# Joining two expert plans into one, with the conditional moved from after the third expert pair to the last heavy expert's first product

## The chip, the cores and the metric

The kernel runs on one core of one Trainium2 chip. The metric is device time in microseconds (us) of one execution. The engines have short names: PE is the matrix engine, DVE the vector engine, ACT the scalar engine, POOL GpSimd, and SP the engine whose queue starts the weight loads.

## What is computed

The program is a two-layer backbone. Layer 0 has attention, a gated convolution and a dense SwiGLU; layer 1 has the same mixing part and then eight experts, of which each token uses two. The change touches only the experts:

```python
def moe_swiglu(h, w_router, w_gu, w_down):
    logits = (h @ w_router).astype(jnp.float32)
    top_v, top_i = lax.top_k(logits, TOP_K)
    top_w = jax.nn.softmax(top_v, axis=-1)
    gates = jnp.sum(jax.nn.one_hot(top_i, N_EXPERTS, dtype=jnp.float32) * top_w[..., None], axis=-2).astype(h.dtype)
    y = jnp.zeros_like(h)
    for e in range(N_EXPERTS):
        y = y + gates[..., e:e + 1] * swiglu(h, w_gu[e], w_down[e])
    return y
```

There are 256 tokens of width 1024; an expert has 1024 x 7168 gate and up weights and 3584 x 1024 down weights in float32, 42 loads of 1 MB each, so that all eight are 336 loads.

## The kernel before, in words

The experts are sorted by how many tokens chose them. The four fullest (ranks 0 to 3) are **heavy**: up to 128 tokens as the stationary operand, and every weight tile is split into a high and a low float32r half, so that one product becomes three (`mm3`, L535 to L537). The four emptiest (ranks 4 to 7) are **light**: up to 64 tokens, and the weights are used as they were loaded (`light_gu`, L1731, and `light_down`, L1799). Rank 1 may have up to 160 tokens. If it has more than 128, the rest of them, the **few**, are multiplied by the unsplit weights as well (L1707 and L1777, tokens prepared in `few_tokens`). A conditional on that count (`k1 > 8 * 128 + 7`, L1888) chooses between two copies of the code, one with the few and one without. The page shows products of L1707, so the copy with the few, which stands first, is the one that runs. An earlier conditional (L1873) guards all of this: its first branch is for other counts of tokens and does not run here; the plans stand in its far branch.

A heavy and a light expert form a pair. `schedule` writes the order of the work: the 3584 columns are cut into four chunks (1024, 1024, 1024, 512), and a step takes gate (`g`) and up (`u`) of one chunk of the heavy and one of the light expert, in turns, then down (`d`) of the chunk before, and the turn (`t`, transposes of the activation). With `LAG_L` = 1 the light expert runs one chunk behind the heavy one. Before the change there are two plans:

```python
HS, LS, LAG_L = (0, 2, 3), (4, 5, 6), 1
plans = [list(schedule(HS, LS, LAG_L)), list(schedule((1,), (7,), 0))]
```

Plan one runs three pairs with the lag, plan two the pair of ranks 1 and 7 without it, behind the conditional. The program order of the plan is kept on PE, DVE and ACT. Loads go through `Mixed`, in the plan's order, into eight raw buffers (`raw`). A heavy weight tile is split by a copy on ACT (`whi`, L99, two halves) and a subtraction on DVE (`wlo`, L100) into one of three buffers of each kind; its raw buffer is then free. A light tile's raw buffer is free when PE has read it, and a tile that the few also need is kept until then. `Wb.ready(2)` after every operation of the plan issues splits until two heavy tiles lie ready, and starts the loads that have become possible. Every engine works its list in order, so where a split stands in the list of ACT or DVE decides what waits behind it.

Small work is put between the operations by `bg_step`: `gather` and `light_gather` fetch the tokens of the next experts (selectors on DVE, products on PE, copies on ACT), and `combine` adds a finished expert into `y` (products on PE, L1359, sums on DVE, L1361). `finish` makes the last sums, the norm and the output.

Of the kernel before, what the change touches and what calls it, by code (L numbers as in the profile page):

```python
# [123 lines left out]
class Mixed(Stream):  # L124

    floor, cap = None, None

# [24 lines left out]
    def get(self, kind):  # L154
        i = self.gi
        assert self.items[i][1] == kind, (kind, self.items[i][1])
        self.load(i + 1)
        self.split(i + 1)
        self.more(i)
        self.gi += 1  # L160
        self.last_raw = self.kept.pop(i, None)
        return self.done.pop(i)
# [3 lines left out]
def kernel(ctx: ExitStack, tc: tile.TileContext, x, c, cx, c_ctx, w_ada, b_ada, norm_g,  # L166
# [855 lines left out]
    def schedule(hs, ls, lag):  # L1022
# [6 lines left out]
        for s in range(n + lag + 1):  # L1029
# [3 lines left out]
            for op in "gu":  # L1033
                for i in range(2):
                    for kind, at in (("H", H), ("L", L)):
                        if i in parts(at):
                            yield kind + op, *at, i
            last = s == n and not lag
            for i in range(2):
                for kind, at, new in (("L", LP, L), ("H", HP, H)) if last else (("H", HP, H), ("L", LP, L)):  # L1040
                    if i in parts(at):
                        yield kind + "d", *at, i
                    if new and i == max(len(parts(at)) - 1, 0):
                        yield kind + "t", *new, 0

    HS, LS, LAG_L = (0, 2, 3), (4, 5, 6), 1
    plans = [list(schedule(HS, LS, LAG_L)), list(schedule((1,), (7,), 0))]

# [566 lines left out]
    def light_gather(p):  # L1615

        n = LS.index(p) if p in LS else 3
        tl_ = ring.tile([128, 512], F32R, "x2", 2 + n % 2)
# [4 lines left out]
        for t in range(2):  # L1623
            V.tensor_scalar(sl[:, t, :].rearrange("p (g n) -> p g n", g=2),
                            iota[:, 0:64].unsqueeze(1).to_broadcast([128, 2, 64]), posms[:, t, p:p + 1], None,
                            op0=OP.is_equal)
        yield
        for h in range(2):
# [16 lines left out]
    def run_pairs(plan, few, todo):  # L1645
# [14 lines left out]
        def few_tokens(p):  # L1660
# [6 lines left out]
            for h in range(2):  # L1667
                pb, q = (facc, lacc)[h], slice(32 * h, 32 * h + 32)
                for i, (t, src) in enumerate(((0, hth), (0, htl), (1, hth), (1, htl))):
# [7 lines left out]
            for t in range(2):  # L1677
                PE.transpose(lb[:, 128 * t:128 * t + 128], sl2[:, t, :].bitcast(F32), ident)
            A.copy(st2, lb[:, :256])
            yield  # L1680
# [55 lines left out]
        def heavy_turn(p, c, i):  # L1736
            n = CHUNKS[c][1]
            for b in range(n // 512):
# [4 lines left out]
                V.tensor_tensor(tl[b], hb[b], th[b].bitcast(F32), op=OP.subtract)  # L1743
            if few:
                for j in range(n // 512):
# [9 lines left out]
        def heavy_down(p, c, i):  # L1755
            nb = CHUNKS[c][1] // 512
            final = c == len(CHUNKS) - 1
            Wb.floor = Wb.gi if few else None
            raws = []
            for t in range(2):  # L1760
# [8 lines left out]
                if final:  # L1769
                    bg_step(2)  # L1770
            if few:
                for t in range(2):
# [7 lines left out]
            if final:  # L1780
                bg_flush()
                OE[p] = split_out(pd)
                parts = [(ST[p], whole(OE[p]))]
                if few:
                    split_hl(th[1], tl[1], facc)
                    parts.append((st2, in_halves((th[1], tl[1]))))
                if p != 1:
                    bg.append(combine(gates[:, :, p], parts, wait=2))
                S_["parts"] = parts

        def light_down(p, c, i):
# [16 lines left out]
        for op, p, c, i in plan:  # L1808
            for f in todo.get((op, p, c, i), ()):
# [71 lines left out]
    with odd_arm.Else():  # L1881
# [6 lines left out]
        with tc.If(k1 > 8 * 128 + 7) as few_arm:  # L1888
            finish(gates[:, :, 1], run_pairs(plans[1], True, {}))
        back1()  # L1890
        with few_arm.Else():
            finish(gates[:, :, 1], run_pairs(plans[1], False, {}))
    touch([k for k in shared if k[0] != "raw"])
# [46 lines left out]
```

## Time and profile before

| | us |
|---|---|
| median of 3 runs | 1942.01 (1940.58 to 1945.11) |
| the profiled execution's own time | 1943.33 |
| its span, first to last instruction | 1941.5 |
| PE busy, share of the span | 1829.9, 94% |
| DVE busy | 947.3, 49% |
| ACT busy | 812.0, 42% |
| main DMA queue | 519.27 MB, 73.5% of 16 engines |

An engine that is busy 94% of the time need not be the limit all along: the stages have different limits, and a row of the trace says for each gap which instruction or transfer ended it. Device time is a little longer than the span, here by 1.8 us, since it also covers what lies before the first and behind the last instruction.

### The profile page before, as it was taken

How to read it: one execution, taken by the hardware profiler on the slowest of the kernel's cores; microseconds unless marked ns; L12 is line 12 of the kernel's file. 1: busy time of each engine (PE TensorE's matmuls, PEld its weight loads, DVE VectorE, ACT ScalarE, POOL GpSimd, SP SyncE). 2: the span in 40 equal slices, each digit the busy share in tenths (PEclk: the TensorE clock that was granted, in tenths of full speed). 3: DMA queues.
4: the chain of work that ended last, by engine and by line, in shares of the span. 5: the costliest groups of instructions: out<-in, count | busy, mean ns of one | idle time of the engine just before them, and what ended most of it. 6: DMA issues, size and time to landing. Idle time of an engine off the chain costs nothing. (4 is left out here: it accounts for less than half of the span.)

```text
span 1941.5 us, 23935 instructions
## 1 busy us (share of the span) xinstructions
PE 1829.9 (94%) x9321; PEld 1277.7 (66%) x9321; DVE 947.3 (49%) x1310; ACT 812.0 (42%) x1194; POOL 79.0 (4%) x139
## 2 busy tenths in 40 slices
PE   6999999999999999999779989999999996999997
PEld 3866679877777888877656646665565653555563
DVE  3345578222223757546745535556355543345443
ACT  3354456221112546446445444444344532244432
POOL 2200110000000000201200000000000000000001
PEclk9999999999999999999779999999999998999999
DMA  9956296545552647634249999999999999799993
GB/s 332 211 171 204 87 313 211 171 151 173 173 174 101 245 153 260 153 99 183 79 156 340 377 383 397 394 406 402 365 405 403 409 404 363 295 358 381 368 365 121
DMA packets 223761, 521.12 MB, mean 268 GB/s; under 512 B 30041, under 2 KB 83857, under 8 KB 223633
## 3 DMA queue, kind: packets, MB, share of 16 engines
q1 hardware_dynamic: 223152, 519.27, 73.5%
q8 instruction: 77, 1.26, 0.3%
q14 instruction: 52, 0.42, 0.1%
q10 hardware_dynamic: 480, 0.18, 0.0%
HBM read 518.31 MB, written 3.13 MB: 269 GB/s over the span
## 5 line engine op out<-in xcount | busy, mean ns | idle before, releaser
L100 DVE TENSOR_TENSOR wlor<-rawr,whir 128x1024 fp32r<-128x1024 f32 x336 | 392.3, 1220 | 310.9 <-ACT whir L99 310.3
L99 ACT CAST whir<-rawr 128x1024 fp32r<-128x1024 f32 x336 | 333.5, 1049 | 254.9 <-DMA rawr<-in_w_down_moe_dram 116.4
L100 DVE TENSOR_TENSOR wlo<-raw,whi 128x1024 fp32r<-128x1024 f32 x188 | 224.8, 1223 | 113.6 <-ACT whi L99 74.5
L99 ACT CAST whi<-raw 128x1024 fp32r<-128x1024 f32 x192 | 193.0, 1049 | 142.3 <-PE pg L536 40.3
L1731 PE MATMUL gur<-rawr,x32r 128*64 128x512 f32 (+1 forms) x1024 | 210.0, 557 | 14.6 <-ACT lar L1753 14.1
L535 PE MATMUL gur<-whir,xgr 128*128 128x512 f32 x448 | 182.5, 407 | 18.9 <-DVE tlr L1743 8.4
L536 PE MATMUL gur<-wlor,xgr 128*128 128x512 f32 x448 | 177.8, 397 | 2.3 <-DVE wlor L100 2.3
L537 PE MATMUL gur<-whir,xgr 128*128 128x512 f32 x448 | 177.0, 395 | 0.0
L1731 PEld LDWEIGHTS gur<-rawr,x32r 128*64 128x64 f32 x1024 | 70.6, 140 | 127.8 <-issue 103.2
L535 PEld LDWEIGHTS gur<-whir,xgr 128*128 128x128 f32 x448 | 85.7, 191 | 56.7 <-issue 18.8
L1799 PE MATMUL pd<-rawr,lar 128*64 128x512 f32 x448 | 101.6, 598 | 1.7 <-ACT lar L1753 1.7
L536 PEld LDWEIGHTS gur<-wlor,xgr 128*128 128x128 f32 x448 | 85.9, 192 | 19.7 <-DVE wlor L100 3.2
L537 PEld LDWEIGHTS gur<-whir,xgr 128*128 128x128 f32 x448 | 85.8, 192 | 18.6
L535 PE MATMUL pg<-hh,whi 128*128 128x512 f32 (+1 forms) x256 | 95.0, 372 | 0.0
L537 PE MATMUL pu<-hh,wlo 128*128 128x512 f32 (+1 forms) x256 | 93.0, 363 | 0.4 <-DVE wlo L100 0.4
L537 PE MATMUL pg<-hh,wlo 128*128 128x512 f32 (+1 forms) x256 | 93.1, 364 | 0.0
L535 PE MATMUL pu<-hh,whi 128*128 128x512 f32 (+1 forms) x256 | 92.9, 363 | 0.0
L536 PE MATMUL pg<-hl,whi 128*128 128x512 f32 (+1 forms) x256 | 92.9, 363 | 0.0
L536 PE MATMUL pu<-hl,whi 128*128 128x512 f32 (+1 forms) x256 | 92.8, 362 | 0.0
L943 DVE TENSOR_TENSOR act<-sg,pu 128x512 f32<-128x512 f32 (+1 forms) x32 | 19.8, 618 | 147.1 <-PE pu L537 128.7
L535 PE MATMUL py<-whi,ah 128*128 128x512 f32 x224 | 87.4, 390 | 0.0
L537 PE MATMUL py<-whi,al 128*128 128x512 f32 x224 | 86.8, 390 | 0.6 <-DVE al L548 0.6
(391 smaller groups left out, 2972.9 us busy)
## 6 DMA issues: line engine op xcount, KB each, us to landing
rawr<-in_w_gu_moe_dram SPq DMA_DIRECT2D x224, 1024.0 KB
rawr<-in_w_down_moe_dram SPq DMA_DIRECT2D x112, 1024.0 KB
raw<-in_w_ada_dram SPq DMA_DIRECT2D x48, 1024.0 KB
raw<-in_w_gu_dense_dram SPq DMA_DIRECT2D x32, 1024.0 KB
raw<-in_w_down_dense_dram SPq DMA_DIRECT2D x28, 1024.0 KB
raw<-in_w_in_dram SPq DMA_DIRECT2D x24, 1024.0 KB
raw<-in_w_out_dram SPq DMA_DIRECT2D x12, 1024.0 KB
BM<-rep SPq DMA_DIRECT2D x8, 512.0 KB
```

The lines of the kernel that those rows point to most:

```text
L99: nc.scalar.copy(hi[:, q], flat[:, q])
L100: (nc.gpsimd if g == "G" else nc.vector).tensor_tensor(lo[:, q], flat[:, q], hi[:, q].bitcast(F32), op=OP.subtract)
L535: PE.matmul(o, wh, mh, start=first, stop=False, skip_group_check=shared)
L536: PE.matmul(o, wh, ml, start=False, stop=False, skip_group_check=shared)
L537: PE.matmul(o, wl, mh, start=False, stop=last, skip_group_check=shared)
L943: V.tensor_tensor(act[f // 4][:, f % 4, s0:s0 + n], sg, pu, op=OP.mult)
L1731: PE.matmul(o[64 * g_:64 * g_ + 64, :], X32[p][:, kk, :], raw[:, k, w2 * g_:w2 * g_ + w2], start=kk == 0, stop=kk == KD - 1)
L1799: PE.matmul(lacc[64 * h:64 * h + 64, :], lt[:, 128 * j + 64 * g_:128 * j + 64 * g_ + 64], raw[:, f, hsl(h)], start=c == 0 and i == t == f ...
```

## The change

There is one plan for all four pairs, `schedule((0, 2, 3, 1), (4, 5, 6, 7), 1)`, cut in two lists at the first product of the last heavy expert. The conditional stands at the cut, so the last chunk of the third pair's light expert, and the down products of both its experts' last chunks, now lie behind the conditional, inside both copies. The last pair runs with the lag.

```diff
-    floor, cap = None, None
+    floor, cap, eager = None, None, False
...
         self.split(i + 1)
+        self.gi += 1
+        if self.eager:
+            self.ready(2)
         self.more(i)
-        self.gi += 1
...
-            last = s == n and not lag
             for i in range(2):
-                for kind, at, new in (("L", LP, L), ("H", HP, H)) if last else (("H", HP, H), ("L", LP, L)):
+                for kind, at, new in (("H", HP, H), ("L", LP, L)):
...
-    HS, LS, LAG_L = (0, 2, 3), (4, 5, 6), 1
-    plans = [list(schedule(HS, LS, LAG_L)), list(schedule((1,), (7,), 0))]
+    HS, LS, LAG_L = (0, 2, 3, 1), (4, 5, 6, 7), 1
+    plan = list(schedule(HS, LS, LAG_L))
+
+    cut = plan.index(("Hg", 1, 0, 0))
+    plans = [plan[:cut], plan[cut:]]
...
-        yield
+        yield from pause(3)
...
-                bg.append(combine(gates[:, :, p], [(SL32[p], in_halves(o))], wait=2 if p != 7 else 0))
+                S_["parts"] = [(SL32[p], in_halves(o))]
+                if p != LS[-1]:
+                    bg.append(combine(gates[:, :, p], S_["parts"], wait=2))
...
-            Wb.ready(2)
-            if op[1] != "t":
+            if after[0][1:] != "t":
+                Wb.ready(3 if op[0] == "L" else 2)
+
+            if op[1] == "d" or op[1] != "t" and not few:
                 bg_step(2 if (p, c) == (0, 0) else 1)
...
-            finish(gates[:, :, 1], run_pairs(plans[1], True, {}))
+            finish(gates[:, :, LS[-1]], run_pairs(plans[1], True, {}))
```

Further small edits go with it: the few are used only where `p == 1`, and their tokens are prepared in the heavy accumulators `hb` and in `facc`, since `lacc` and `lb` now hold the light expert's sums at that time; the heavy expert of rank 1 is combined in the background, and the light one of rank 7 in `finish`.

Splits move in three ways. After a light operation up to three heavy tiles are made ready, not two. No split is issued between an operation and a turn that follows it. In the first chunk of the first heavy expert (`eager`) splits are issued inside the products. The gather of the light tokens pauses for three more operations behind its selectors, and with the few the background work advances only behind down products.

**On ACT, at the conditional** (`thr` and `lar` are the turned activations of heavy and light, `whi` the split's high half, `rawr_7094` the raw buffer of the 245th load in both kernels). Before, from the last heavy down products' tiles on:

```order
L99 CAST whir_7102<-rawr_7096 128x1024 x2
L99 CAST whir_7216<-rawr_7094 128x1024 x2
L99 CAST whir_7385<-rawr_7096 128x1024 x2
L1742 CAST thr_7405<-gur_7409 128x512
L1753 COPY lar_7396<-gur_7411 128x512
L1720 ACTIVATE sgr_7401<-gur_7411 128x256
L547 CAST oer_7397<-pdn0r_7412 128x512
L547 CAST oer_7397<-pdn1r_7413 128x512
L99 CAST whir_7102<-rawr_7094 128x1024 x2
```

Now, up to the few's tokens (`sgr_7402`):

```order
L99 CAST whir_7102<-rawr_7096 128x1024 x2
L99 CAST whir_7216<-rawr_7086 128x1024 x2
L1746 CAST thr_7405<-gur_7409 128x512
L99 CAST whir_7385<-rawr_7088 128x1024 x2
L1757 COPY lar_7396<-gur_7411 128x512
L99 CAST whir_7102<-rawr_7094 128x1024 x2
L1895 COMPARE_AND_BRANCH
L1675 COPY sgr_7402<-gur_7409 32x512
L1675 COPY sgr_7402<-gur_7410 32x512
```

Both turns now stand ahead of that split; the conditional and the copies of the few's tokens stand behind it. The DVE list has the same order: the split's low half, the conditional, then the selectors of the few.

**On ACT, in the first heavy expert's first chunk** (`actr` is its activated gate, `x2f` the gathered light tokens). Before:

```order
L99 CAST whir_7102<-rawr_7092 128x1024 x2
L1632 COPY x2f<-pd_7383 64x512
L1720 ACTIVATE actr_7403<-gur_7409 128x512
L1720 ACTIVATE actr_7404<-gur_7410 128x512
L99 CAST whir_7216<-rawr_7094 128x1024 x2
L99 CAST whir_7385<-rawr_7096 128x1024 x2
L1632 COPY x2f<-tr_7382 64x512
L1637 CAST x2r_7392<-pd_7383 128x256
```

Now:

```order
L99 CAST whir_7102<-rawr_7092 128x1024 x2
L99 CAST whir_7216<-rawr_7094 128x1024 x2
L99 CAST whir_7385<-rawr_7096 128x1024 x2
L1724 ACTIVATE actr_7403<-gur_7409 128x512
L1724 ACTIVATE actr_7404<-gur_7410 128x512
L1636 COPY x2f<-pd_7383 64x512
L99 CAST whir_7102<-rawr_7098 128x1024 x2
L99 CAST whir_7216<-rawr_7100 128x1024 x2
```

Two tiles are split ahead of the gate's activation that were split behind it, and the copy of the light tokens moved behind it.

**On PE, at the second light gather** (`pd_7383` receives the gathered tokens, `gur_7411` is the light accumulator). Before, between two operations of the plan:

```order
L1731 MATMUL gur_7411<-rawr_7098,x32r_7394 64x512 x4
L1731 MATMUL gur_7411<-rawr_7100,x32r_7394 64x512 x4
L1631 MATMUL pd_7383<-hth,x2r_7393 128x512
L1631 MATMUL pd_7383<-htl,x2r_7393 128x512
L1631 MATMUL pd_7383<-hth,x2r_7393 128x512
L1631 MATMUL pd_7383<-htl,x2r_7393 128x512
L1731 MATMUL gur_7411<-rawr_7086,x32r_7394 64x512 x4
L1731 MATMUL gur_7411<-rawr_7088,x32r_7394 64x512 x4
```

Now:

```order
L538 MATMUL gur_7409<-wlor_7386,xgr_7387 128x512
L539 MATMUL gur_7409<-whir_7385,xgr_7387 128x512
L1635 MATMUL pd_7383<-hth,x2r_7393 128x512
L1635 MATMUL pd_7383<-htl,x2r_7393 128x512
L1635 MATMUL pd_7383<-hth,x2r_7393 128x512
L1635 MATMUL pd_7383<-htl,x2r_7393 128x512
L1735 MATMUL gur_7411<-rawr_7094,x32r_7394 64x512 x4
L1735 MATMUL gur_7411<-rawr_7096,x32r_7394 64x512 x4
```

The four products stand three operations further on, behind the next heavy gate or up products; their selectors on DVE stayed where they were.

## Rows read from the trace of the kernel before

**Rows 1.** The page's 40 slices of the span (48.5 us each): TensorE, then the DMA engines.
```profile
PE   6999999999999999999779989999999996999997
...
DMA  9956296545552647634249999999999999799993
```

**Rows 2.** Stretches of 50 us: us, PE, PEld, DVE, ACT, POOL busy, clock, DMA share, GB/s.
```profile
1300.00:1350.00 50.00, 50.00 (x222) 30.11 (x221) 25.44 (x25) 20.40 (x25) 0.00 (x0) 1.00 1.02 400
1600.00:1650.00 50.00, 34.89 (x178) 19.50 (x175) 15.78 (x15) 13.31 (x15) 0.00 (x0) 0.83 0.94 365
1650.00:1700.00 50.00, 46.23 (x242) 25.42 (x242) 18.53 (x24) 14.99 (x21) 0.00 (x0) 0.97 0.77 296
1750.00:1800.00 50.00, 50.00 (x289) 29.31 (x287) 26.91 (x27) 21.51 (x24) 0.00 (x0) 1.00 0.98 378
```

**Rows 3.** Timeline, PE, between the two plans: start, length, work, [idle before <- releaser].
```profile
1624.13 0.65 PE L1752 MATMUL gur<-kc,sgr 128*128 128x128 f32 x4
1638.87 6.11 PE L1731 MATMUL gur<-rawr,x32r 128*64 128x256 f32 x32 [14.08 <-ACT lar L1753]
...
1663.92 3.65 PE L1799 MATMUL pd<-rawr,lar 128*64 128x512 f32 x16 [1.23 <-ACT lar L1753]
...
1669.67 0.73 PE L1359 MATMUL pd<-oer,str 128*128 128x512 f32 x2 [0.95 <-DVE y L1361]
...
1674.78 0.80 PE L1670 MATMUL pd<-hth,x2r 128*128 128x512 f32 x1 [1.23 <-DVE p L1664]
```

**Rows 4.** Timeline, ACT, the same stretch.
```profile
1612.27 1.99 ACT L99 CAST whir<-rawr 128x1024 fp32r<-128x1024 f32 x2 [5.70 <-DMA rawr<-in_w_down_moe_dram]
...
1633.30 1.99 ACT L99 CAST whir<-rawr 128x1024 fp32r<-128x1024 f32 x2 [16.49 <-DMA rawr<-in_w_down_moe_dram]
1635.85 1.99 ACT L99 CAST whir<-rawr 128x1024 fp32r<-128x1024 f32 x2 [0.56 <-DMA rawr<-in_w_down_moe_dram]
...
1638.23 0.59 ACT L1753 COPY lar<-gur 128x512 f32<-128x512 f32 x1
```

**Rows 5.** Timeline, DVE: last split of plan one, first selector behind the conditional.
```profile
1634.38 2.36 DVE L100 TENSOR_TENSOR wlor<-rawr,whir 128x1024 fp32r<-128x1024 f32 x2 [16.12 <-ACT whir L99]
...
1674.26 0.14 DVE L1664 TENSOR_SCALAR p<-posms 128x1 f32<-128x1 f32 x1
```

**Rows 6.** Timeline, PE: the waits of the first pairs.
```profile
1000.22 0.50 PE L536 MATMUL gur<-wlor,xgr 128*128 128x512 f32 x1 [0.75 <-DVE wlor L100]
...
1017.55 0.79 PE L535 MATMUL gur<-whir,xgr 128*128 128x512 f32 x1 [4.48 <-DVE tlr L1743]
...
1147.92 0.79 PE L1631 MATMUL pd<-hth,x2r 128*128 128x512 f32 x1 [5.91 <-DVE x2r L1624]
...
1371.36 0.80 PE L1631 MATMUL tr<-hth,x2r 128*128 128x512 f32 x1 [4.20 <-DVE x2r L1624]
```

**Rows 7.** Stretches of 10 us around those waits, columns as in rows 2.
```profile
1010.00:1020.00 10.00, 5.39 (x22) 3.81 (x21) 9.01 (x10) 3.89 (x5) 0.00 (x0) 0.79 0.76 278
1150.00:1160.00 10.00, 10.00 (x39) 5.67 (x40) 0.00 (x0) 3.75 (x5) 0.00 (x0) 0.88 0.81 306
1370.00:1380.00 10.00, 8.64 (x24) 3.51 (x25) 1.50 (x3) 1.18 (x2) 0.00 (x0) 0.66 0.71 261
```

**Rows 8.** Timeline, PE, the end of the last pair.
```profile
1909.04 3.65 PE L1799 MATMUL pd<-rawr,lar 128*64 128x512 f32 x16 [0.47 <-ACT lar L1753]
...
1919.07 0.73 PE L1359 MATMUL tr<-x2r,x2r 64*128 64x512 f32 x2 [0.84 <-DVE y L1361]
...
1925.18 1.19 PE L1359 MATMUL gur<-oer,str 128*128 128x512 f32 x4
```

**Rows 9.** Timeline, ACT: a gate, and the split that is queued behind it.
```profile
1138.46 0.60 ACT L1720 ACTIVATE actr<-gur 128x512 f32<-128x512 f32 x1 [6.00 <-PE gur L537]
1141.53 1.99 ACT L99 CAST whir<-rawr 128x1024 fp32r<-128x1024 f32 x2 [2.47 <-DMA rawr<-in_w_gu_moe_dram]
```

**Rows 10.** Timeline, PE: the first product behind the first conditional.
```profile
982.43 0.80 PE L535 MATMUL gur<-whir,xgr 128*128 128x512 f32 x1 [6.80 <-issue]
```

More of the change, by code (lines that the diff above doesn't have):

```diff
@@ L1615, in light_gather @@
     def light_gather(p):
-        n = LS.index(p) if p in LS else 3
+        n = LS.index(p)
         tl_ = ring.tile([128, 512], F32R, "x2", 2 + n % 2)
@@ L1667, in few_tokens @@
             for h in range(2):
-                pb, q = (facc, lacc)[h], slice(32 * h, 32 * h + 32)
+                pb, q = hb[h], slice(32 * h, 32 * h + 32)
                 for i, (t, src) in enumerate(((0, hth), (0, htl), (1, hth), (1, htl))):
@@ L1677, in few_tokens @@
             for t in range(2):
-                PE.transpose(lb[:, 128 * t:128 * t + 128], sl2[:, t, :].bitcast(F32), ident)
-            A.copy(st2, lb[:, :256])
+                PE.transpose(facc[:, 128 * t:128 * t + 128], sl2[:, t, :].bitcast(F32), ident)
+            A.copy(st2, facc[:, :256])
             yield
@@ L1743, in heavy_turn @@
                 V.tensor_tensor(tl[b], hb[b], th[b].bitcast(F32), op=OP.subtract)
-            if few:
+            if few and p == 1:
                 for j in range(n // 512):
@@ L1757, in heavy_down @@
             final = c == len(CHUNKS) - 1
-            Wb.floor = Wb.gi if few else None
+            Wb.floor = Wb.gi if few and p == 1 else None
             raws = []
@@ L1770, in heavy_down @@
                     bg_step(2)
-            if few:
+            if few and p == 1:
                 for t in range(2):
@@ L1783, in heavy_down @@
                 parts = [(ST[p], whole(OE[p]))]
-                if few:
+                if few and p == 1:
                     split_hl(th[1], tl[1], facc)
                     parts.append((st2, in_halves((th[1], tl[1]))))
-                if p != 1:
-                    bg.append(combine(gates[:, :, p], parts, wait=2))
-                S_["parts"] = parts
+                bg.append(combine(gates[:, :, p], parts, wait=1 if p == 1 else 2))
         def light_down(p, c, i):
@@ L1803, in light_down @@
                 split_hl(*o, lacc)
-                bg.append(combine(gates[:, :, p], [(SL32[p], in_halves(o))], wait=2 if p != 7 else 0))
+                S_["parts"] = [(SL32[p], in_halves(o))]
+                if p != LS[-1]:
+                    bg.append(combine(gates[:, :, p], S_["parts"], wait=2))
         code = nc.cur_bb.bb.instructions
         n = len(code)
-        for op, p, c, i in plan:
+        for (op, p, c, i), after in zip(plan, plan[1:] + [("", 0, 0, 0)]):
+            Wb.eager = (p, c) == (0, 0)
             for f in todo.get((op, p, c, i), ()):
@@ L1888 @@
         with tc.If(k1 > 8 * 128 + 7) as few_arm:
-            finish(gates[:, :, 1], run_pairs(plans[1], True, {}))
+            finish(gates[:, :, LS[-1]], run_pairs(plans[1], True, {}))
         back1()
         with few_arm.Else():
-            finish(gates[:, :, 1], run_pairs(plans[1], False, {}))
+            finish(gates[:, :, LS[-1]], run_pairs(plans[1], False, {}))
     touch([k for k in shared if k[0] != "raw"])
```

## The prediction

> **What bounds the kernel now.** I read the page's slices first: from the 22nd slice on (about 1020 us) PE and the DMA engines are both at 9 or above, with one dip on PE at the 34th [rows 1]. That is the stage of the experts, the only one that the change touches. So the second view is busy time by stretch. In 1300 to 1350 PE is busy all the time and the DMA share is 1.02 at 400 GB/s: two limits of nearly the same height. In 1600 to 1700 PE loses 15.1 and 3.8 us and the DMA share falls to 0.77. From 1750 on PE is full and the DMA share is 0.98 at 378 GB/s: there PE is the limit, since the last pair also multiplies the few [rows 2].
>
> The third view is the timeline at the border of the two plans. PE ends the last light turn of plan one at 1624.13 + 0.65 and waits until 1638.87, for `lar`, a copy on ACT [rows 3]. The copy itself is short. It stands behind the splits of two tiles that had not landed: ACT waited 16.49 us for the first, cast it at 1633.30, the second at 1635.85, and only then came the turns [rows 4]. By the plan (three pairs of 84 loads, the last 12 of them light 4, heavy 2, light 6) these tiles are loads 245 and 246. Load 237, eight buffers before, was cast at 1612.27 [rows 4]: 21.0 us for eight loads is 2.63 us each, which is the DMA engines at their full pace. So up to the border the loads set the time, and PE waits for them wherever it gets ahead; behind it PE does, with hardly a gap up to 1909 [rows 8].
>
> The rule for the sum follows: ahead of the conditional only what lets loads start sooner counts; behind it, every microsecond that PE stands idle, and the moment at which it starts.
>
> **The restart at the border.** The new plan has the same 240 loads ahead of the cut, and the 245th, now the third tile of the last heavy expert, lands in the same place of the order. The turns move ahead of its split, but so does nothing else: split, conditional and the few's selectors and tokens follow in this order on ACT and DVE, and PE's next work is the tokens. With loads as before, the cast is at 1633.30, DVE ends the low half at 1634.38 + 2.36 = 1636.74 [rows 4, 5]. The first token product came 0.52 us after the first selector started (1674.78 against 1674.26) [rows 3, 5], so PE restarts at 1637.3, not 1638.87: **1.6 us gained**, where the diff looks as if it took away the whole wait of 14.08 [rows 3]. From here to the last product PE has the same products to make in either plan: light chunk, down products, tokens, the last pair. They only stand in another order.
>
> **The handshakes behind it.** Before, the combines of ranks 3 and 6 were flushed at the border, PE and DVE in turns, and then came the conditional and the tokens: waits of 1.23, 0.95 and 1.23 us [rows 3]. At the end 0.47 and 0.84 belong to the light turn and the combine of rank 7 among heavy products [rows 8]. Together 4.7 us. The eight parts of the two combines now stand singly behind down products. Their price is nothing if DVE's sum ends within the next down products, and 8 x 0.95 = 7.6 us if each waits as the one in the row did. I take 1.0, near nothing, because the next products of such a group are longer than the wait. **3.7 us gained.** In the tail the light combine of rank 7 now comes behind the last product where the heavy one of rank 1 was [rows 8]. There are four sums on DVE and the same norm in either case, so I put it at nothing, between a gain and a loss of 1.
>
> **The start.** In the first chunk PE waits 0.75 us for a low half and then 4.48 us for a turned activation's low half [rows 6]. The second stands on DVE behind splits that were issued between the products and the turn; these splits no longer go there, and the first is what the eager splits remove. In 1010 to 1020 the DMA share is 0.76 [rows 7]: the raw buffers are full and the loads follow PE, so what PE gains here the loads gain too. **5.0 us** of the 5.2. The ends are nothing, if the loads are held up again right after, and 8, if the clock of 0.79 in that stretch [rows 7] stays full as well.
>
> **The light gathers.** Twice PE stands at a gather's first product for a selector, 5.91 and 4.20 us [rows 6], because DVE built it behind the splits of tiles that had yet to land. Three operations later the selector is long done, so both waits go. But these stretches are bound by loads: what counts is the dip that follows, when PE had not freed the light buffers. The shares 0.81 and 0.71 against 1.02 are (0.21 + 0.31) x 10 = **5.2 us** [rows 2, 7]. The ends are nothing and the 10.1 us of the waits. The postponed copies are needed only when the next light expert starts, and that lies behind the rest of the step.
>
> The third tile ready after a light operation, and turns ahead of splits, cost nothing in themselves: the same casts in another order, on ACT and DVE which are half idle (in 1300 to 1350 busy 20.40 and 25.44 of 50 us) [rows 2].
>
> **Sum.** 1.6 + 3.7 + 5.0 + 5.2 = 15.5 us, so the profiled execution's 1943.33 would become 1927.8. That execution is 1.3 above the median of 1942.01; against the median I say **1926.5**. The loads' 10.2 us shift load 245, and with it the restart, to about 1627; the wait at the cut remains some 12 us long.
>
> **The rivals.**
> The loads don't gain. If the ring of eight buffers is held up at the next place, the two load terms are worth nothing, and 1.6 + 3.7 = 5.3 leaves 1936.7. For it: the share was 1.02 in most stretches, so a later bottleneck has little to give back. Against it: a dip in a full ring is time that nothing returns.
>
> More comes than that. If the third ready tile lets raw buffers go earlier all along, the upper ends count: 8 + 10.1 instead of 10.2, some 8 us more, 1918.5.
>
> Slower: a split in front of the gate. After a light operation the third split now stands ahead of the heavy gate's activation on ACT. In the trace a gate ran at 1138.46 and the split behind it waited 2.47 us for its load, to be cast in 1.99 up to 1143.52 [rows 9]. In the other order the gate would have been 1143.52 - 1138.46 = 5.1 us late. PE then waits for the accumulator that the gate empties, and the light buffers behind it go free later. The point from which it decides is three of the stage's some twelve steps, since 3 x 5.1 = 15.3 us eats the whole gain; if six steps lose that much, 6 x 5.1 - 15.5 = 15.1 us slower, about 1957. Against it: the up products that need the accumulator use that very tile, so PE mostly waits for it anyway.
>
> The conditional itself costs. At the first conditional, whose far branch runs, PE stood 6.80 us with no releaser in the profile [rows 10]; at the second one the gap of 1.23 ended with DVE's selector [rows 3], so I price it at nothing. If a gap like the first one came behind the wait at the cut, 1926.5 + 6.8 = 1933.3. The Trainium skill, "Runtime: NRT & Kernel Launch", section on instruction fetch mechanics, says that a taken branch to code outside the present window waits until that code is fetched. By that rule the jump into the far copy pays and falling into the near one does not; the trace agrees for both conditionals, 6.80 against none.
>
> **How the numbers follow.** Forecast 0.60 (its own range 1919 to 1933); loads don't gain 0.18 (1933 to 1940); more 0.10; slower 0.06; the conditional 0.06. A measurement of this kernel can tell about 0.2% from no change, 3.9 us, so faster means under 1938.1. The forecast, the larger gain and the conditional give 0.76 nearly whole, the second case about half: faster 0.85. Same has 0.08, the rest of the second case, and slower 0.07, the slower case and a little for losses that I have not seen. The range, 1916 to 1938, leaves out half of the larger gain (0.05), the part of the second case above 1938 (0.08) and the slower case (0.06), about 0.19.
>
> **What would show it.** Right: at the border one wait of PE, about 12 us, ended by DVE's selectors, with ACT's cast of the last split before the conditional near 1623; no wait for a selector at the gathers, and none over 2 us near 1015; shares near 1.02 where they were 0.81 and 0.71; PE without gaps from the tokens on. Wrong: the cast at the cut still near 1633 (the loads gained nothing), no wait at the cut (PE was the limit after all), gates on ACT behind a split that waits for a load while PE stands, or new gaps at the combines.

## The result, and the profile after

The changed kernel takes **1917.28 us** (median of 4 runs, 1915.79 to 1919.9), the kernel before in the same comparison 1943.56 us (1940.58 to 1947.96): a ratio of **0.9866, 95% interval 0.9845 to 0.9887**. The profiled execution of after took 1916.19 us with a span of 1914.4, against 1943.33 and 1941.5 before: 27.1 us less, where the sum said 15.5. In the changed file the lines lie a few numbers further down: a light product of L1731 is now L1735, down L1799 is L1801, the turns L1742 and L1752 are L1746 and L1756, the few's selectors L1664 are L1668, their token products L1670 are L1674, a combine's L1359 and L1361 are L1363 and L1365, and the split's L535 to L537 are L537 to L539.

The page's slices of after:

```profile
PE   6999999999999999999779999999999996999997
...
DMA  9956286645552656733438999999999998898994
```

The dip of PE at the 34th slice is still there, the smaller one at the 24th is gone [rows 1]. The DMA digits of this stage were 9 before as well: slices of 48 us hide the short dips of the loads. Stretches, with the columns of rows 2, around the waits of the gathers and of the border:

```profile
1150.00:1160.00 10.00, 7.15 (x27) 4.39 (x24) 5.23 (x5) 4.47 (x5) 0.00 (x0) 0.83 1.03 409
1370.00:1380.00 10.00, 7.83 (x36) 5.03 (x32) 4.80 (x5) 4.51 (x6) 0.00 (x0) 1.00 1.02 407
1610.00:1620.00 10.00, 0.00 (x0) 0.00 (x0) 4.67 (x7) 2.70 (x4) 0.00 (x0) 0.50 0.97 386
1620.00:1630.00 10.00, 9.91 (x38) 7.57 (x38) 0.38 (x3) 1.23 (x3) 0.00 (x0) 0.83 0.11 43
```

At the gathers the shares of 0.81 and 0.71 [rows 7] became 1.03 and 1.02, and no stretch of 10 us from 1100 to 1180 or from 1340 to 1400 is below 1.02, so the dips have not only moved. The last two rows show the border: the loads run on at 0.97 while PE does nothing, and fall to 0.11 once it goes on. That is what full raw buffers would look like: from here PE is the limit.

PE from the last light turn before the conditional, after:

```profile
1607.20 0.66 PE L1756 MATMUL gur<-kc,sgr 128*128 128x128 f32 x4
1620.09 0.80 PE L1674 MATMUL gur<-hth,x2r 128*128 128x512 f32 x1 [12.24 <-DVE p L1668]
1620.68 0.63 PE L1674 MATMUL gur<-htl,x2r 128*128 128x512 f32 x1
...
1623.60 0.40 PE L537 MATMUL gur<-whir,xgr 128*128 128x512 f32 x1
```

ACT there:

```profile
1608.23 1.99 ACT L99 CAST whir<-rawr 128x1024 fp32r<-128x1024 f32 x2
1610.13 0.58 ACT L1757 COPY lar<-gur 128x512 f32<-128x512 f32 x1
1616.21 1.99 ACT L99 CAST whir<-rawr 128x1024 fp32r<-128x1024 f32 x2 [5.51 <-DMA rawr<-in_w_gu_moe_dram]
```

And DVE:

```profile
1617.29 2.36 DVE L100 TENSOR_TENSOR wlor<-rawr,whir 128x1024 fp32r<-128x1024 f32 x2 [5.29 <-ACT whir L99]
1619.57 0.15 DVE L1668 TENSOR_SCALAR p<-posms 128x1 f32<-128x1 f32 x1
```

The light turn's copy `lar`, for which PE waited before [rows 3], is done at 1610.13 + 0.58. What PE now waits for is the selector behind the low half of the third tile, which landed late (ACT waited 5.51 us for it): its cast runs at 1616.21, where before it ran at 1633.30 [rows 4]. That is 17.1 us earlier. PE restarts at 1620.09 instead of 1638.87, 18.8 earlier; the 1.7 beyond the cast are the 1.6 of the forecast.

PE's remaining waits over 0.2 us behind the restart:

```profile
1743.71 0.50 PE L537 MATMUL gur<-whir,xgr 128*128 128x512 f32 x1 [0.56 <-DVE tlr L1747]
...
1868.08 3.67 PE L1735 MATMUL gur<-rawr,x32r 128*64 128x256 f32 x32 [0.68 <-ACT lar L1757]
1873.04 3.67 PE L1735 MATMUL gur<-rawr,x32r 128*64 128x256 f32 x32 [1.28 <-ACT sgr L1724]
1894.90 3.65 PE L1801 MATMUL pd<-rawr,lar 128*64 128x512 f32 x16 [0.46 <-ACT lar L1757]
```

They are 0.56 + 0.68 + 1.28 + 0.46 = 2.98 us. The restart to the end of the span took 1941.5 - 1638.87 = 302.6 us before and 1914.4 - 1620.09 = 294.3 now. So of the 27.1 us some 18.8 came ahead of the restart and 8.3 behind it.

At the start and at the first gather, where rows 6 had 4.48 and 5.91, PE's timeline of after has:

```profile
982.42 0.79 PE L537 MATMUL gur<-whir,xgr 128*128 128x512 f32 x1 [6.71 <-issue]
...
1013.09 0.50 PE L537 MATMUL gur<-whir,xgr 128*128 128x512 f32 x1 [0.81 <-DVE tlr L1747]
...
1155.23 0.44 PE L1640 MATMUL pd<-kc,x2r 128*128 128x128 f32 x2 [2.85 <-ACT x2f L1636]
...
1372.90 0.44 PE L1640 MATMUL tr<-kc,x2r 128*128 128x128 f32 x2 [1.00 <-ACT x2f L1636]
1380.59 0.66 PE L1645 MATMUL pd<-kc,x2f 128*128 128x128 f32 x4 [1.76 <-ACT x2f L1636]
```

At the gathers no product waits for a selector any more, but some wait for `x2f`, the copies of the gathered tokens. ACT's timeline ahead of the first such wait:

```profile
1150.12 2.00 ACT L99 CAST whir<-rawr 128x1024 fp32r<-128x1024 f32 x2 [10.52 <-DMA rawr<-in_w_down_moe_dram]
1152.70 1.99 ACT L99 CAST whir<-rawr 128x1024 fp32r<-128x1024 f32 x2 [0.59 <-DMA rawr<-in_w_down_moe_dram]
1154.60 0.57 ACT L1636 COPY x2f<-pd 64x512 f32<-64x512 f32 x1
```

The copy stands behind two splits that wait for loads. With 0.28 us at 1163.02 these waits are 2.85 + 0.28 + 1.00 + 1.76 = 5.89 us.

The first product starts at 982.42, as before [rows 10], so the tile casts of the two profiles can be compared as they stand. Taking the cast of the same heavy tile on ACT in both timelines, after is 7.5 us ahead at the 16th tile, 7.8 at the 32nd, 9.2 at the 40th, 10 to 14 from the 46th to the 75th, 16.2 at the 82nd, and 16 to 18 from the 99th to the cut; single tiles whose place in the order changed stand out by up to 10. The first step is the first chunk's, the later ones lie where the light gathers and the turns are.

### The profile page after: what moved, and what is told of

It reads as the page before. It is cut to its first block, busy times and chain, and to the rows that moved or that the text cites. A ratio compares the mean times of both kernels' runs of the same rounds, so it can differ in the third digit from the quotient of the medians.

```text
span 1914.4 us, 23955 instructions
## 1 busy us (share of the span) xinstructions
PE 1818.3 (95%) x9321; PEld 1273.7 (67%) x9321; DVE 948.4 (50%) x1310; ACT 812.2 (42%) x1194; POOL 79.0 (4%) x139
## 5 line engine op out<-in xcount | busy, mean ns | idle before, releaser
L1735 PE MATMUL gur<-rawr,x32r 128*64 128x512 f32 (+1 forms) x1024 | 205.1, 547 | 6.5 <-ACT lar L1757 5.3
L537 PE MATMUL gur<-whir,xgr 128*128 128x512 f32 x448 | 181.0, 404 | 11.8 <-issue 6.7
L539 PE MATMUL gur<-whir,xgr 128*128 128x512 f32 x448 | 175.6, 392 | 0.0
L1735 PEld LDWEIGHTS gur<-rawr,x32r 128*64 128x64 f32 x1024 | 69.5, 137 | 118.2 <-issue 100.0
L537 PEld LDWEIGHTS gur<-whir,xgr 128*128 128x128 f32 x448 | 84.9, 190 | 51.1 <-issue 22.0
L1801 PE MATMUL pd<-rawr,lar 128*64 128x512 f32 x448 | 101.7, 598 | 0.5 <-ACT lar L1757 0.5
L539 PEld LDWEIGHTS gur<-whir,xgr 128*128 128x128 f32 x448 | 84.8, 189 | 18.4
L537 PE MATMUL pg<-hh,whi 128*128 128x512 f32 (+1 forms) x256 | 95.0, 372 | 0.0
L539 PE MATMUL pu<-hh,wlo 128*128 128x512 f32 (+1 forms) x256 | 93.0, 363 | 0.4 <-DVE wlo L100 0.4
L539 PE MATMUL pg<-hh,wlo 128*128 128x512 f32 (+1 forms) x256 | 93.1, 364 | 0.0
L537 PE MATMUL pu<-hh,whi 128*128 128x512 f32 (+1 forms) x256 | 92.9, 363 | 0.0
L537 PE MATMUL py<-whi,ah 128*128 128x512 f32 x224 | 87.4, 390 | 0.0
L539 PE MATMUL py<-whi,al 128*128 128x512 f32 x224 | 86.8, 390 | 0.6 <-DVE al L550 0.6
```

Source lines behind the costliest of these rows:

```text
L537: PE.matmul(o, wh, mh, start=first, stop=False, skip_group_check=shared)
L539: PE.matmul(o, wl, mh, start=False, stop=last, skip_group_check=shared)
L1735: PE.matmul(o[64 * g_:64 * g_ + 64, :], X32[p][:, kk, :], raw[:, k, w2 * g_:w2 * g_ + w2], start=kk == 0, stop=kk == KD - 1)
L1801: PE.matmul(lacc[64 * h:64 * h + 64, :], lt[:, 128 * j + 64 * g_:128 * j + 64 * g_ + 64], raw[:, f, hsl(h)], start=c == 0 and i == t == f ...
```

## The experiments

Two questions were open: why the loads came 17 us forward and not 10, and where 8.3 us behind the restart came from. Theory A was that the new rules for splits (`eager`, no split before a turn, three ready, the pause) give the 17 us, that the joined plan gives the 8.3, and that the two add up. What rivals say is told in each expectation. For comparing profiles, one table cuts every profiled span at three points: the first expert product, the restart (the first product behind the long wait at the border or the cut), and the end. The start itself varies between profiles by up to 9 us, so the last two columns are what to read:

```
kernel                 start    restart   start to restart   restart to end
before                982.43    1638.87        656.4             302.6
after                 982.42    1620.09        637.7             294.3
c_after               985.21    1623.11        637.9             295.4
e6_rules_only         981.19    1619.98        638.8             308.4
e7_join_only          981.29    1627.01        645.7             308.4
e1_no_eager           976.27    1615.48        639.2             294.3
e2_early_gather       984.89    1628.69        643.8             294.4
e3_two_ready          981.86    1623.02        641.2             302.3
e9_split_before_turn  984.57    1629.70        645.1             305.8
e4_cut_two            982.17    1610.82        628.7             295.3
e4b_cut_two           984.26    1613.15        628.9             295.3
e8_no_conditional     976.71    1605.16        628.5             293.4
e10_cut_one           978.86    1605.55        626.7             294.1
```

**The changed kernel again (c_after)**, no edit.

> The changed kernel as it is, for comparison on the same chip: 0.9866 of the kernel before within its interval, near 1917 us.

1917.03 us, ratio 0.9855 (0.9825 to 0.9886) to before's 1944.54. The result repeats, and so do both columns, to 0.2 and 1.1 us.

**The rules without the joined plan (e6_rules_only)**: the kernel before with its two plans, plus

```diff
-    floor, cap = None, None
+    floor, cap, eager = None, None, False
...
         self.split(i + 1)
-        self.more(i)
         self.gi += 1
+        if self.eager:
+            self.ready(2)
+        self.more(i)
...
-        yield
+        yield from pause(3)
...
+            Wb.eager = (p, c) == (0, 0)
...
-            Wb.ready(2)
+            if after[0][1:] != "t":
+                Wb.ready(3 if op[0] == "L" else 2)
```

> The two plans as before, with only the rules for splits and gathers changed (eager first chunk, three tiles ready after a light operation, no split ahead of a turn, later light gathers). Theory A: the 17 us by which load 245 came earlier are the rules' work, and the border and what follows stay as before. So load 245 is cast near 1616, PE still waits some 13 us at the border for the light turn's copy and restarts near 1622, and the time is about 17 us shorter than before, 1926. Rival B: the joined plan brought the loads forward; then load 245 is cast within 4 us of 1633 and the time is above 1937.

1932.02 us, ratio 0.9941 (0.992 to 0.9961): 12.5 us better than before, not the expected 17. The stretch up to the restart is what A said, 656.4 - 638.8 = 17.6 us shorter. Behind it 308.4 - 302.6 = 5.8 us were lost. PE's timeline of this run, at the border and at the flush of the combines behind it:

```profile
1619.98 6.47 PE L1733 MATMUL gur<-rawr,x32r 128*64 128x256 f32 x32 [13.53 <-ACT lar L1755]
...
1655.58 1.22 PE L1361 MATMUL pd<-oer,str 128*128 128x512 f32 x2 [5.32 <-DVE y L1363]
```

DVE's timeline of this run says why:

```profile
1646.53 0.75 DVE L1363 SCALAR_TENSOR_TENSOR y<-tr,gates,y 128x512 f32<-128x512 f32 x1
1651.91 2.36 DVE L100 TENSOR_TENSOR wlor<-rawr,whir 128x1024 fp32r<-128x1024 f32 x2 [4.63 <-ACT whir L99]
...
1654.79 0.74 DVE L1363 SCALAR_TENSOR_TENSOR y<-pd,gates,y 128x512 f32<-128x512 f32 x1
```

The third split stands ahead of the combine's sums, waits 4.63 us for its tile, and PE at the flush waits for the sum, 5.32 us where it waited 0.95 before [rows 3]. With the two plans the rules thus lose at the border part of what they gain ahead of it; in the joined plan no flush stands there.

**The joined plan without the rules (e7_join_only)**:

```diff
-        yield from pause(3)
+        yield
...
-            Wb.eager = (p, c) == (0, 0)
+            Wb.eager = False
...
-            if after[0][1:] != "t":
-                Wb.ready(3 if op[0] == "L" else 2)
+            Wb.ready(2)
```

> The joined plan with the old rules (two tiles ready after every operation, turns included, no eager chunk, light gathers at once). Theory A: loads come as before the change, but only loads up to 242 are split ahead of the conditional, some 8 us before load 245, so PE restarts near 1630 instead of 1639, and with the 8 us that the stretch behind the conditional saved the time is about 17 us shorter than before, 1926. Rival B: the join brings the loads forward too: below 1920. Rival C: the old rules keep PE waiting at the cut for load 245 as before: 1935.

1934.65 us, ratio 0.9951 (0.9937 to 0.9964): 9.9 us better than before, against 17 expected. The tile casts ahead of the cut came only 1.4 us forward, as A said. PE restarts after 645.7 us instead of 656.4, since the conditional now stands behind two tiles. But the stretch behind it took 308.4 us, 14 more than in after. PE's timeline of this run:

```profile
1015.35 0.80 PE L537 MATMUL gur<-whir,xgr 128*128 128x512 f32 x1 [4.49 <-DVE tlr L1747]
...
1652.86 0.49 PE L537 MATMUL gur<-whir,xgr 128*128 128x512 f32 x1 [1.55 <-ACT whir L99]
1654.12 0.79 PE L538 MATMUL gur<-wlor,xgr 128*128 128x512 f32 x1 [0.77 <-DVE wlor L100]
1675.65 0.50 PE L538 MATMUL pdn0r<-wlor,thr 128*128 128x512 f32 x1 [1.25 <-DVE wlor L100]
...
1887.39 6.18 PE L1735 MATMUL gur<-rawr,x32r 128*64 128x256 f32 x32 [5.96 <-ACT lar L1757]
```

and ACT's, ahead of the last of them:

```profile
1882.31 1.99 ACT L99 CAST whir<-rawr 128x1024 fp32r<-128x1024 f32 x2 [4.36 <-DMA rawr<-in_w_down_moe_dram]
1884.87 1.99 ACT L99 CAST whir<-rawr 128x1024 fp32r<-128x1024 f32 x2 [0.57 <-DMA rawr<-in_w_down_moe_dram]
1886.77 0.58 ACT L1757 COPY lar<-gur 128x512 f32<-128x512 f32 x1
```

The light copy stands behind two splits that wait for loads. The 32 light products behind the wait then took 6.18 us instead of 3.67. So A's sum fell: the parts alone give 12.5 and 9.9, both 27.5. These medians alone would hardly tell 22.4 from 27.5, but the table does, in both columns. Ahead of the restart the parts give 17.6 and 10.7, and both together 18.5, far less than the sum of 28.3: with the rules it is a third tile's split that stands ahead of the conditional, and with two tiles there (e4_cut_two, below) it is 27.7, near the sum. Behind it each alone loses 5.8, and both together gain 7.2 to 8.3: each removes a stall that the other alone leaves open.

**Without the eager splits (e1_no_eager)**: `Wb.eager = False`.

> The changed kernel without the eager splits in the first chunk. Theory A: what the start gave (loads some 7 us earlier from 1060 us on) comes from the turn that no longer stands behind splits, and the eager splits alone carry only the waits of 0.49 and 0.75 us: the time rises by 1 to 2 us to about 1918.5, and the casts of the 20th heavy tile and later come 1 to 2 us later. Rival: the eager splits start the loads and carry most of the 7 us: about 1923.

1918.49 us, ratio 0.9887 (0.9854 to 0.9919). Measured from its own start, the restart came 1.5 us later, and nothing changed behind it. The 4.48 us wait of rows 6 did not come back. Its four times lie in two pairs, 1911.61 and 1913.91, 1923.07 and 1923.23, so the median tells little, and only the column shows the difference.

**The gather without its pause (e2_early_gather)**: `yield` in place of `yield from pause(3)`.

> The changed kernel with the light gathers at once again, instead of three operations behind their selectors. Theory A: waits of PE of 4 to 6 us for a selector come back near 1140 and 1360, the loads lose the 5.2 us of the two dips, and the time rises by 5 to about 1922. Rival: with three tiles ready and the ring of raw buffers used better the waits are hidden, and the time stays within 2 us of 1917.

1921.67 us, ratio 0.9888 (0.9861 to 0.9915). Start to restart is 6.1 us longer, and PE waits at both gathers' first products again:

```profile
1144.08 0.79 PE L1635 MATMUL pd<-hth,x2r 128*128 128x512 f32 x1 [7.35 <-DVE x2r L1628]
...
1363.79 0.79 PE L1635 MATMUL tr<-hth,x2r 128*128 128x512 f32 x1 [5.52 <-DVE x2r L1628]
```

These two are 12.9 us of PE's time, and the stretch lost half of that. But the 5.89 us that after waits for the copies at the same gathers are gone here, so the net at these two gathers is 7.0. The loads dip again too, to shares of 0.85 (1140 to 1150) and 0.87 (1360 to 1370): against 1.02 that is 3.2 us, and 4.8 with the stretches up to 1170 and 1390.

**Two tiles ready after every operation (e3_two_ready)**; at the cut three, as in after:

```diff
-                Wb.ready(3 if op[0] == "L" else 2)
+                Wb.ready(2 if after[0] else 3)
```

> The changed kernel with two heavy tiles ready after light operations too, except at the cut, where it stays three. Theory A: the third tile is what I had priced at nothing and gave the remaining 5 us of the loads: load 245 is cast some 5 us later than in the changed kernel, and the time is about 1922. Rival: the order of casts on a half idle ACT costs nothing either way, and the time stays within 2 us of 1917.

1926.74 us, ratio 0.9924 (0.99 to 0.9948): 9.7 us over c_after's median, 5 more than expected. The table parts it: 3.5 us ahead of the restart and 8.0 behind. Behind it PE's timeline shows five waits, such as

```profile
1648.11 0.50 PE L537 MATMUL gur<-whir,xgr 128*128 128x512 f32 x1 [1.55 <-ACT whir L99]
1649.37 0.50 PE L538 MATMUL gur<-wlor,xgr 128*128 128x512 f32 x1 [0.76 <-DVE wlor L100]
1669.60 0.50 PE L538 MATMUL pdn0r<-wlor,thr 128*128 128x512 f32 x1 [1.25 <-DVE wlor L100]
```

The others are 1.53 and 0.76 at 1752.07 and 1753.33; together 5.85 us. In after none of them is there. In the stretch where PE is the limit, the third tile spares it the wait for cast and subtraction of a tile that has landed: ACT began that cast at 1647.02 without waiting for a load. The rest shows when the stretch from the restart to the plan's last product is cut out, in before, after and this run (columns as in rows 2):

```profile
1638.87:1925.25 286.38, 278.99 (x1722) 160.55 (x1722) 125.15 (x131) 102.70 (x126) 0.00 (x0) 0.99 0.85 326
1620.09:1898.55 278.46, 275.39 (x1722) 159.75 (x1722) 120.89 (x123) 100.77 (x124) 0.00 (x0) 0.99 0.87 336
1623.02:1909.51 286.49, 278.15 (x1722) 161.26 (x1722) 119.98 (x123) 100.23 (x124) 0.00 (x0) 0.99 0.85 326
```

PE makes the same 1722 products in all three. Here it was idle 8.34 us (286.49 - 278.15) against 3.07 in after, 5.27 more, and busy 2.76 us longer with the same work. Together these are the 8.0.

**Splits in front of turns again (e9_split_before_turn)**: the condition on the next operation is gone, three and two ready as in after.

```diff
-            if after[0][1:] != "t":
-                Wb.ready(3 if op[0] == "L" else 2)
+            Wb.ready(3 if op[0] == "L" else 2)
```

> The changed kernel with splits made ready between an operation and a turn that follows it, as before. Theory A: the waits for a turned activation's low half come back, 4.5 us near 1015 and about 6 us at the turn of the last pair's last chunk: the loads lose 5 us, PE 6 more behind the cut, and the time is about 1928. Rival: only the start loses, 1922.

1937.45 us, ratio 0.9968 (0.9951 to 0.9984): 20 us over c_after's median, more than any other part, and 9 more than expected. From 637.7 to 645.1 the stretch ahead of the restart grew by 7.4, the one behind it by 11.5. The wait at the first chunk's turn, where I had expected it, did not come back (0.80 at 1015.12). It came at the light turns, of which A had named only the one in the last pair's last chunk. PE and ACT at the first of them:

```profile
1138.42 9.89 PE L1735 MATMUL gur<-rawr,x32r 128*64 128x512 f32 x32 [5.63 <-ACT lar L1757]
```

```profile
1135.90 1.99 ACT L99 CAST whir<-rawr 128x1024 fp32r<-128x1024 f32 x2 [9.98 <-DMA rawr<-in_w_gu_moe_dram]
1137.79 0.58 ACT L1757 COPY lar<-gur 128x512 f32<-128x512 f32 x1
```

The copy that PE needs stands 0.58 us long behind a cast that waits 9.98 us for its load. The same wait is 6.14 at 1359.01, 5.62 at 1578.56 and 5.03 at 1887.89; at 1832.89 PE waited 2.82 for a combine's sum that stood behind a split on DVE. Eager splits and turns ahead of splits each suffice against the 4.48 of rows 6: with either one left out, it stayed away, and with both left out (e7) it is there again, 4.49.

**Two tiles ready at the cut (e4_cut_two, e4b_cut_two)**: `and after[0]` added, so the third tile is not split ahead of the conditional.

```diff
-                Wb.ready(3 if op[0] == "L" else 2)
+                Wb.ready(3 if op[0] == "L" and after[0] else 2)
```

> The changed kernel with two heavy tiles instead of three made ready at the cut, so that the few's selectors on DVE no longer stand behind the split of load 245. Theory A: the 12.24 us wait at the cut is a matter of that order alone; the selectors follow the split of load 242 (over at 1612.0), PE restarts at 1612.5 instead of 1620.1, and since PE sets the time from there all 7.6 us stay: about 1909.7. Rival: loads 245 to 250 come too late for the earlier start, PE waits in the last heavy expert's first gate products instead, and the time stays above 1914.

> The same kernel as in the run with two tiles ready at the cut, beside the next one on the same chip: near 1909, 0.9824 of the kernel before within its interval.

1909.04 us, ratio 0.9824 (0.9795 to 0.9852), and on another occasion 1910.25, 0.9825 (0.9786 to 0.9864). The wait at the cut fell from 12.24 to

```profile
1610.82 0.80 PE L1674 MATMUL gur<-hth,x2r 128*128 128x512 f32 x1 [4.33 <-DVE p L1668]
```

and start to restart by 9.0 us, with 1.0 given back behind. This shows that the remaining wait was the place of the third split, and that an earlier restart counts nearly whole.

**One tile ready at the cut (e10_cut_one)**:

```diff
-                Wb.ready(3 if op[0] == "L" else 2)
+                Wb.ready(1 if not after[0] or (op, p, c) == ("Ht", HS[-2], 3) else 3 if op[0] == "L" else 2)
```

The second condition keeps the last heavy turn ahead of the cut from making the second tile ready.

> As the run before, with one heavy tile ready at the cut, so that the selectors stand ahead of the split of load 242 as well. Theory A: of the wait at the cut, 4.33 us with two tiles, some 2.4 go (one split's low half on DVE), and the second tile's split still ends about when PE comes to it: about 1907. Rival: PE waits those 2 us for the second tile instead, 1909.

**1905.06 us**, ratio 0.9804 (0.9764 to 0.9844), the fastest that keeps both copies. Its four times, 1901.72 to 1907.73, lie below all of the changed kernel's (the lowest, in c_after, is 1912.24). The wait is 2.09 us, and start to restart 11.0 shorter than in after, nothing given back. Against e4b, of the same occasion, it is 5.2 us lower, of which the table explains 3.4; the profiled start, at 978.86, was also early.

**Without the second conditional (e8_no_conditional)**: only the copy with the few is built, so that the kernel lacks the one for up to 128 tokens.

```diff
-        with tc.If(k1 > 8 * 128 + 7) as few_arm:
-            finish(gates[:, :, LS[-1]], run_pairs(plans[1], True, {}))
-        back1()
-        with few_arm.Else():
-            finish(gates[:, :, LS[-1]], run_pairs(plans[1], False, {}))
+        finish(gates[:, :, LS[-1]], run_pairs(plans[1], True, {}))
```

> The changed kernel without the conditional: only the copy with the few is left (the copy for 128 tokens or fewer is left out). Theory A: the conditional costs nothing, since its near branch falls through and every engine's list goes on; PE still waits some 12 us for the selectors behind the split of load 245, and the time is within 2 us of the changed kernel's 1917. Rival: some of the wait at the cut or of the work behind it is the conditional's price, up to 6.8 us: 1910 to 1913.

1901.16 us, ratio 0.9775 (0.9731 to 0.9819): 16 us below after, where I had expected 2 at most. It was to price the conditional, and it changed the order instead. Without it the selectors, which need nothing from the experts, stand at the very start of the expert part on DVE, and the copies of the tokens stand ahead of the last split on ACT. PE then restarts with

```profile
1605.16 0.50 PE L1674 MATMUL gur<-hth,x2r 128*128 128x512 f32 x1 [1.73 <-DVE tlr L1747]
```

So the stretch up to the restart is 9.2 us shorter, near the 9.0 and 11.0 of e4 and e10, and the one behind it 0.9, which lies in the tail: from the last product of an expert to the end it is 14.6 us here and 15.9 in after. The rest of the 16 is the start, which is 5.7 earlier in this profile. In the expert stage, then, what the conditional costs is mostly that nothing behind it can be placed ahead of the split before it. Its own price was not separated, and whether the left-out copy has to do with the early start is open.

## Why the prediction held, and which terms were mis-sized

The direction held, and so did the range, 1917.28 in 1916 to 1938, by 1.3 us. The case did not: 1917.28 lies below the forecast's own range of 1919 to 1933, where only the case of a larger gain stood, with a chance of 0.10. The point was 9 us high; the sum said 15.5 and the profiles say 27.1. Term by term:

**The restart, 1.6: right.** 18.8 us of the restart's advance less 17.1 of the cast's is 1.7. The wait at the cut stayed, 12.24 us, ended by DVE's selectors, as forecast. The cast before it came at 1616.21, not near 1623.

**The start, 5.0: low.** The casts were 7.5 us ahead at the 16th tile and 7.8 at the 32nd, near the upper bound of 8. The bound came from the clock of 0.79 in that stretch [rows 7], which is 1.00 after: the 4.48 us wait also slowed the products behind it. I named that and took the lower value.

**The light gathers, 5.2: near in size, the reading not separated.** e2 gives 6.1 to the pause. The dips of the DMA share went, as forecast. But "both waits go" was half right: the waits for selectors (10.1) went, and 5.89 us for the postponed copies came, which I had thought to be needed only by the next light expert. PE's net waits, 7.0 in e2, and the dips of the loads, 4.8, lie on either side of 6.1, so the runs don't tell which of them set the price.

**"The third tile ready after a light operation, and turns ahead of splits, cost nothing in themselves": the step that failed.** I priced both at nothing, as loss and as gain, since ACT and DVE were half idle. The runs priced what is lost when one of them is left out: the third tile 3.5 us ahead of the restart and 8.0 behind it (e3), turns ahead of splits 7.4 and 11.5 (e9). An engine that is idle half of the time because it waits inside its list at a split is not free for what stands behind. The prediction used this very argument for the start and for the gathers, and not for the light turns. In before I could have seen it at one place only: PE waited for `lar` at the border, 14.08 us [rows 3], and 0.47 at most at a light turn within a pair [rows 8]. With two tiles ready and splits in front of turns e7 has one large wait of this kind in the whole stage, with three tiles e9 has four of 5.03 to 6.14. So it seems that the third tile makes the rule on turns necessary, and that e9 is so dear for that reason; e7 lacks the eager splits and the pause as well, so this is argued and not shown. Nor does the rule remove all of it. In after two light turns still wait, as their copy stands behind a split that an earlier operation issued (idle 5.64 and 5.67 us for its load); e3, with two tiles, has neither:

```profile
1229.75 5.35 PE L1735 MATMUL gur<-rawr,x32r 128*64 128x512 f32 x16 [2.29 <-ACT lar L1757]
...
1447.32 3.65 PE L1735 MATMUL gur<-rawr,x32r 128*64 128x512 f32 x16 [2.29 <-ACT lar L1757]
```

The loads' part closes nearly: eager 1.5, pause 6.1, third tile 3.5, turns 7.4 are 18.5, against 17.0 to 18 of the casts in after. These prices are each for one part taken out of the whole, and they overlap at the start and at the light turns, so that the sum comes out so close is partly luck.

**The handshakes behind the restart, 3.7: low, 8.3 measured.** The waits went from 7.0 us (nine of 0.23 to 1.23, the largest in rows 3 and 8) to 2.98, or 4.1, near the forecast. What I left out stands in rows 3: after the wait of 14.08 the 32 light products took 6.11 us at a granted clock of 0.59 (1638.87 to 1644.98), against 3.67 at 1.00 in after (1868.08), or 2.4 more. Before, the slow clock was paid at these products and a second time at the tokens (1674.78, 0.80 for one product); after, only at the tokens, 8 of 0.8 to 0.5 us. The stretches cut out above close the sum: up to the last product PE was idle 7.39 us before and 3.07 now, 4.3 less, and busy 278.99 and 275.39 with the same 1722 products, 3.6 less, of which the 2.4 are the largest part. The tail gave 0.4, inside its 1, and 4.3 + 3.6 + 0.4 = 8.3.

**The rivals.** "The loads don't gain" fell: the casts moved by 17.1. "More comes than that", 1918.5, hit the time, and its condition, that the third ready tile lets raw buffers go earlier all along, is partly shown by e3; more than half of what the third tile gives lies behind the restart, though, where loads are no limit. "A split in front of the gate" did happen as an order: nine gates in after stand right behind a split that waited 3.2 to 10.0 us for its load, where before two did, behind 1.2 and 2.3. It cost next to nothing. The gate behind the longest wait on ACT:

```profile
1569.46 1.99 ACT L99 CAST whir<-rawr 128x1024 fp32r<-128x1024 f32 x2 [9.99 <-DMA rawr<-in_w_gu_moe_dram]
1571.36 0.59 ACT L1724 ACTIVATE actr<-gur 128x512 f32<-128x512 f32 x1
```

PE waited 0.66 us for it (1572.00), and for none of the other eight over 0.2. My argument against this case was not the reason, though: PE did not stand waiting for that tile, it had other products to make. The first of the nine ran at 1136.30, when PE was busy with light products up to 1137.45. A related wait, of the light turn behind a split, is what e9 shows, and the change's own rule avoids most of it. "The conditional itself costs" did not happen either: PE restarted at 1620.09, 0.52 us after the first selector began on DVE (1619.57), the same 0.52 as before [rows 3, 5], without an "issue" gap; DVE, whose selectors end the wait, began them with no idle time behind the split (1617.29 + 2.36). That fits the Trainium skill, "Runtime: NRT & Kernel Launch", section on instruction fetch mechanics, which ties the fetch stall to a taken branch whose target lies outside the present window. A stall of PE itself could hide under its wait, but before that wait was only 1.23 us [rows 3]. No run here tells how much of the first conditional's gap is that stall.

## What to carry to other kernels

Where every engine works its list in order, price a moved split (or any instruction that waits for a load) by what stands behind it in the list and who waits for that, even if the engine is idle half of the time. Preparing more ahead and keeping short handovers in front of what waits belong together: without the third tile the kernel was 9.7 us slower, without the rule on turns 20. Measure groups of edits alone and together: the rules and the joined plan gave 12.5 and 9.9 us alone and 27.5 together. A conditional was a fence for the order here (e8); what is issued just ahead of it decides when everything behind it starts, so issue there only what has already landed.

## What was not expected of the hardware

The gap at the first conditional, in which PE waits for nothing that the profile shows, is not one number: 6.80 us before and 6.71 after, but 3.58 in e8, 4.07 in e1 and 4.40 in e10. The first product came at 976.27 to 985.21 in the profiles, two of the three earliest starts from kernels that keep all code (e1, e10), so the amount of code does not explain it. One thing goes with it: in e1, e8 and e10 the last four products `pd<-slr,htl` ahead of the gap (L1337 before, L1341 after) took 0.74 us at a granted clock of 1.00, in all others 1.22 or 1.23 at 0.50, and there the gap is 5.69 to 6.80. Whether the clock makes the gap long, or both follow from something earlier, no run shows. Differences of a few us between single profiles should be taken from a common point behind it.

The price of a wait is more than the wait: the same 32 light products took 3.67 us at full clock, and 6.11, 6.47 and 6.18 us behind idle times of 14.08, 13.53 and 5.96 us (before, e6, e7). A wait of 1.28 us (1873.04 in after) left them at 3.67. The length of the wait alone does not tell: behind two waits of 2.29 us in after, 16 larger light products took 5.35 us at a granted clock of 0.68 and 3.65 at 1.00 (1229.75 and 1447.32).
